# A first stage in quarters: mixed scale and shift chunks, and one-column sums of squares

## The chip, the cores and the metric

One core of a Trainium2 chip runs the whole program: one launch, one inference step. The metric is device time in microseconds (us), the median of repeated runs. A profiled execution of the same program gives the trace from which all durations here are read. Engines are named TensorE (PE; its weight loads are listed as PEld), VectorE (DVE), ScalarE (ACT), GpSimd (POOL) and SyncE (SP, which issues the DMAs of this kernel).

## The reference

One layer of a hybrid decoder, over 1024 prompt tokens and 8 x 4 sample tokens, width 1024, all in float32. What matters here is its beginning, which is the same for prompt and samples:

```
mod = silu(c) @ w_ada + b_ada                      # c: 1 prompt row + 8 sample rows
shift, scale, gate = split(mod, 3)
h = x * rsqrt(mean(x*x) + eps) * g_norm * (1 + scale) + shift
z = h @ w_in                                       # split into mq mk mv, gates, aq ak av, ...
```

After it come an mLSTM branch (q, k, v, two gates per head), an attention branch with a window of 128 and sinks (aq, ak, av), two output products gated by sigmoids of z, the residual with `gate`, and a final norm.

## The kernel before

Tokens lie transposed: `xT[p][k]` is a tile of 128 channels (k = 0..7) by 512 tokens (p = 0, 1), and `xS` holds the 32 sample tokens of all eight k. The matrix `w_in` is used in jobs of 128 columns; `order` lists the jobs, ak and av first, then the four aq. A product is done in a split form: h is kept as a rounded part `h_hi` and a rest `h_lo`, the weights as `wh` and `wl`, and each step of k is three products (wh with h_hi, wh with h_lo, wl with h_hi) that accumulate in PSUM. The columns of tokens are cut in three pieces, `PIECES` (384, 384, and 256 with the 32 samples).

The first stage makes h and, as far as h is ready, the jobs ak and av. Its parts:

- `ada_load`, `ada_rows`, `ada_chunk` (names of tiles: early_h, early_l, ada_, adas_, adat_): one chunk is 512 of the 3072 columns of w_ada, 2 MB. Sixteen passes in four column groups give 512 columns of scale or shift for nine rows, a ScalarE copy brings them to SBUF (`adas`), and four products with a selection matrix turn them (`adat`). Two chunks are scale (sc0, sc1) and two shift (sh0, sh1), each for half of the channels. `scale_done` makes `A` = (1 + scale) * g_norm, `shift_done` makes `B` = shift + bias, for nine rows.
- `x_sq` (xsq, xs, xsum): squares of each token tile, on VectorE and ScalarE in turn, and products with ones that add them over channels in four column groups; a copy to `xsum`.
- `x_rs` (xc, ssq, xr): nine products turn the sums into columns of 128 tokens, and a Newton chain of twelve small VectorE steps (`recip_sqrt`) gives the factors.
- `x_dg`, `x_rows` (xdg, xb): diagonal matrices of the factors and products with ones give each token's factor in all 128 partitions, in PSUM.
- `x_mul`: token tile times A times factor row, one VectorE step; `h_part`: h_hi by adding B (ScalarE, some on VectorE), h_lo on VectorE; `h_plain`: the unsplit h, for the gate products and for storing in DRAM (`hD`); `h_samples`: the same for the samples, with eight small steps for A and B.
- `pair` does the three products of ak and av for some k and one piece; `pair_end` takes the sums out (kr, krr, vT). `gate_piece` (gg) does the eight gate columns from the unsplit h.

The order in the stage is written out by hand in L1511 to L1585. `mm` and `in_order` hold TensorE to it, and the wrappers `V` and `S` hold VectorE and ScalarE to program order as long as their `on` is set; the DMAs stand in program order in one queue with eight outstanding. Behind the stage a planner (`Side`) interleaves attention and gate work with the jobs by due times that are counted in the program, not measured. L213 in the profile is the wrapper's call, L251 `mm`, L239 the DMA issue.

The stage works in halves of k: all sums first, then sc0 and sh0, products of k = 0..3 for the three pieces, with sc1 and sh1 between them, then k = 4..7.

Of the kernel before, what the change touches and what calls it, by code (L numbers as in the profile page):

```python
# [81 lines left out]
def job_columns():  # L82
# [14 lines left out]
    return cols, np.arange(mi, mi + 8), np.concatenate([pair(g) for g in range(4)])  # L97

# [68 lines left out]
def body(tc, a):  # L167
    nc = tc.nc
    with ExitStack() as ctx:
# [100 lines left out]

        cst = cp.tile([128, C_END], F32, name="cst")
        dma(cst[:, :C_TRI], a["cst"][:, :C_TRI])
        ident = cst[:, C_ID:C_ID + 128]
# [4 lines left out]
        cT = ht([128, KT, 9], "cT")  # L278
        dma(cT, a["cT"])
        vec = cp.tile([128, 28], F32, name="vec")  # L280
        dma(vec, a["vec"])
        gmn, bada, gnorm = vec[:, 0:4], vec[:, 4:20], vec[:, 20:28]

        def load_x(p):
            ts = []
            for k in range(KT):
                ts.append(ht([128, 512], f"x{p}_{k}"))
                dma(ts[-1], a["xT"][:, p, k])
            return ts

        xS = ht([128, KT, NS], "xS")
        dma(xS, a["xS"])
        xT = [load_x(p) for p in range(2)]
        xT.append([xS[:, k] for k in range(KT)])

        ct = ht([128, KT, 9], "ct")
        S.activation(ct, cT, AF.Tanh, scale=0.5)
        V.scalar_tensor_tensor(ct, ct, 1.0, cT, op0=ALU.add, op1=ALU.mult)
        c32 = cp.tile([128, KT, 32], F32, name="c32")
        V.memset(c32, 0.0)  # L300
        V.tensor_scalar(c32[:, :, 0:9], ct, 0.5, None, op0=ALU.mult)
# [37 lines left out]
        V.tensor_scalar(b1, bada[:, 8:16], 1.0, None, op0=ALU.add)  # L339
        V.tensor_scalar(gmn, gmn, 0.5, None, op0=ALU.mult)  # L340

        def bc9(v, j):
            return v[:, 4 * j:4 * j + 4].unsqueeze(2).to_broadcast((128, 4, 9))

        def scale_done(j):
# [6 lines left out]
        def shift_done(j):  # L352
            return lambda tp: V.tensor_tensor(B[:, 4 * j:4 * j + 4], tp, bc9(bada[:, 0:8], j), op=ALU.add)

        hD = dp.tile([128, KT, T], F32, name="hD")
        one = cp.tile([128, 128], F32, name="one")
        V.memset(one, 1.0)

        PARTS = (0, 512), (512, 512), (SEQ, NS)

        def x_sq(p):
            n = PARTS[p][1]
            acc = po([128, 512], f"xs{p}")
# [3 lines left out]
            for k in range(KT):  # L367
                if p == 2:
                    sq = sqs[:, k]
                else:  # L370
                    sq = ht([128, 512], "xsq")
                    if k % 2:
                        V.tensor_tensor(sq, xT[p][k], xT[p][k], op=ALU.mult)
                    else:
                        S.activation(sq, xT[p][k], AF.Square)
                j = 32 * (k % 4)
                mm(acc[j:j + 32, :n], one[:, 0:32], sq, start=(k < 4), stop=(k >= 4), share=4)
            sums = ht([128, 512], "xsum")
            S.copy(sums[:, :n], acc[:, :n])
            return sums  # L380

        def x_rs(ps_, sums):
            blocks = [(p, i, min(128, PARTS[p][1])) for p in ps_ for i in range(-(-PARTS[p][1] // 128))]
            nb = len(blocks)
            cols = pg([128, nb], f"xc{ps_[0]}")
            for j, (p, i, m) in enumerate(blocks):
                mm(cols[:m, j:j + 1], sums[p][:, i * 128:i * 128 + m], cst[:, C_S9:C_S9 + 1], start=True, stop=True)
# [99 lines left out]
        def h_hi(k, c0, n, x="h"):  # L487
            ks = k
            if isinstance(k, slice):
                k, ks = k.start, slice(0, 4)  # L490
# [1355 lines left out]
```

## Time and profile before

| | |
|---|---|
| median of 3 runs | 883.22 us (882.14 to 883.58) |
| the profiled execution | 886.0 us, its span 884.2 us |
| TensorE busy | 846.2 us, 96% of the span |
| VectorE, ScalarE, GpSimd busy | 544.3, 381.6, 202.7 us |
| HBM | 106.02 MB read, 39.51 MB written |

The stage in stretches of 5 us (busy us of each engine in the stretch):

| stretch | TensorE | VectorE | ScalarE | DMA, GB/s |
|---|---|---|---|---|
| 5 to 10 | 4.04 | 1.39 | 1.75 | 299 |
| 15 to 20 | 5.00 | 1.48 | 1.92 | 408 |
| 25 to 30 | 4.29 | 3.77 | 0.92 | 392 |
| 30 to 35 | 2.86 | 3.30 | 4.66 | 412 |
| 45 to 50 | 5.00 | 3.76 | 1.95 | 284 |
| 50 to 55 | 3.80 | 4.43 | 5.00 | 32 |
| 60 to 65 | 5.00 | 4.05 | 2.00 | 306 |

How to read the rows of the profile: "start, length, engine, line, operation, out<-in, shapes, count [idle time before it <- what ended that]". Times are us from the start of the span. In rows of a tile the three durations are minimum, median and maximum in ns. In rows of a stretch stand its limits, its length, TensorE's busy time with the number of instructions, the granted clock (1.00 is full), the DMA share and GB/s. Rows of one kind are merged, and their length is then from the first start to the last end or the busy time. A float32 product takes two passes, and each pass is a row of its own.

### The profile page before, as it was taken

The numbers are of one execution on the slowest core, as the hardware profiler recorded it, in microseconds if no ns is written. First come the engines' busy times: TensorE is split into PE (matmuls) and PEld (weight loads), VectorE is DVE, ScalarE is ACT, GpSimd is POOL, SyncE is SP. The second block draws the span as 40 slices with busy tenths as digits, with TensorE's granted clock in tenths as the row PEclk, the third lists the DMA queues.
The fourth block names the chain that finished last, engine by engine and source line by source line (L and its number), as shares of the span: only waits on it lengthen the run. The fifth ranks groups of instructions, "written<-read, shape, count | busy, mean of one in ns | idle before, by whom it ended". The sixth has DMA issues, their size and how long they took to land. (4 is left out here: it accounts for less than half of the span.)

```text
span 884.2 us, 15518 instructions
## 1 busy us (share of the span) xinstructions
PE 846.2 (96%) x5306; PEld 715.8 (81%) x5306; DVE 544.3 (62%) x1496; ACT 381.6 (43%) x986; POOL 202.7 (23%) x208
## 2 busy tenths in 40 slices
PE   6899989999999889999999999999999999999996
PEld 2689988888889879888878877777788999987775
DVE  3786564444758867535655554558756666747785
ACT  3663334445445454645545453434434333223231
POOL 0112210000023423224322223255443302120000
PEclk9999999999999998999999999999999999999998
DMA  8965638364667443344443334464424788452421
GB/s 314 371 227 167 219 128 274 113 223 125 182 164 225 158 127 107 118 161 149 113 136 115 104 124 119 145 174 140 123 93 127 254 284 300 151 155 101 150 78 49
DMA packets 113771, 145.55 MB, mean 165 GB/s; under 512 B 27004, under 2 KB 72444, under 8 KB 113660
## 3 DMA queue, kind: packets, MB, share of 16 engines
q1 hardware_dynamic: 113692, 144.56, 50.7%
q8 instruction: 42, 0.69, 0.3%
q14 instruction: 37, 0.30, 0.1%
HBM read 106.02 MB, written 39.51 MB: 165 GB/s over the span
## 5 line engine op out<-in xcount | busy, mean ns | idle before, releaser
L213 ACT ACTIVATE p<-p,nmx 128x256 f32<-128x256 f32 (+1 forms) x64 | 30.9, 484 | 36.2 <-DVE nmx L213 36.2
L251 PE MATMUL g_w_ao<-ya,wh_w_ao 128*128 128x384 f32 (+1 forms) x192 | 45.5, 322 | 0.9 <-ACT bw L213 0.5
L251 PE MATMUL g_w_mo<-ym_l,wh_w_mo 128*128 128x384 f32 (+1 forms) x192 | 45.7, 323 | 0.0
L213 DVE CUSTOM_DVE_ANT_0 p<-sc,cst,sink 128x256 f32<-128x256 f32 (+1 forms) x64 | 26.1, 463 | 21.7 <-PE sc L251 21.6
L251 PEld LDWEIGHTS g_w_ao<-ya,wh_w_ao 128*128 128x128 f32 x192 | 33.4, 188 | 1.6 <-ACT bw L213 1.0
L213 ACT ACTIVATE fjk<-rows_l 128x512 bf16<-128x512 f32 (+2 forms) x19 | 11.6, 609 | 51.4 <-DVE rows_l L213 25.5
L251 PE MATMUL g_mk<-h_h,wh_mk 128*128 128x384 f32 (+1 forms) x96 | 33.7, 351 | 0.0
L251 PEld LDWEIGHTS g_w_mo<-ym_l,wh_w_mo 128*128 128x128 f32 x192 | 33.5, 188 | 0.0
L251 PE MATMUL g_mv<-h_h,wh_mv 128*128 128x384 f32 (+1 forms) x96 | 33.0, 344 | 0.0
L251 PE MATMUL g_aq<-h_h,wh_aq 128*128 128x384 f32 (+1 forms) x96 | 32.9, 343 | 0.0
L251 PE MATMUL g_mq<-h_h,wh_mq 128*128 128x384 f32 (+1 forms) x96 | 32.5, 338 | 0.0
L251 PE MATMUL g_mk<-h_l,wh_mk 128*128 128x384 f32 (+1 forms) x96 | 31.8, 331 | 0.0
L251 PE MATMUL g_aq<-h_l,wh_aq 128*128 128x384 f32 (+1 forms) x96 | 31.7, 331 | 0.0
L251 PE MATMUL g_mk<-h_h,wl_mk 128*128 128x384 f32 (+1 forms) x96 | 31.6, 329 | 0.0
L251 PE MATMUL g_aq<-h_h,wl_aq 128*128 128x384 f32 (+1 forms) x96 | 31.6, 329 | 0.0
L251 PE MATMUL g_mq<-h_h,wl_mq 128*128 128x384 f32 (+1 forms) x96 | 31.0, 323 | 0.0
L251 PE MATMUL g_mv<-h_h,wl_mv 128*128 128x384 f32 (+1 forms) x96 | 31.0, 323 | 0.0
L251 PE MATMUL g_mq<-h_l,wh_mq 128*128 128x384 f32 (+1 forms) x96 | 31.0, 323 | 0.0
L251 PE MATMUL g_mv<-h_l,wh_mv 128*128 128x384 f32 (+1 forms) x96 | 31.0, 323 | 0.0
L251 PE MATMUL g_w_mo<-ym_l,wl_w_mo 128*128 128x384 f32 (+1 forms) x96 | 31.0, 323 | 0.0
L251 PE MATMUL g_w_ao<-ya,wl_w_ao 128*128 128x384 f32 (+1 forms) x96 | 30.8, 321 | 0.0
L720 POOL TENSOR_TENSOR aq<-aq,cos 128x384 f32<-128x384 f32 (+1 forms) x12 | 15.1, 1254 | 50.2 <-DVE ropet L213 34.5
(1320 smaller groups left out, 2744.3 us busy)
## 6 DMA issues: line engine op xcount, KB each, us to landing
x<-xT SPq DMA_DIRECT2D x16, 256.0 KB, 5.5
early_h<-w_ada SPq DMA_DIRECT2D x8, 512.0 KB, 7.8
early_l<-w_ada SPq DMA_DIRECT2D x8, 512.0 KB, 9.7
hD<-x SPq DMA_DIRECT2D x16, 256.0 KB, 3.3
adar_ga<-w_ada SPq DMA_DIRECT2D x16, 256.0 KB, 5.7
wr_ga<-w SPq DMA_DIRECT2D x16, 256.0 KB, 2.8
hb<-hD SPq DMA_DIRECT2D x16, 256.0 KB, 5.5
wr_gm<-w SPq DMA_DIRECT2D x16, 256.0 KB, 3.1
```

The costliest lines, as they stand in the source:

```text
L213: ins = f(*args, **kw)
L251: in_order(nc.tensor.matmul(out, lhsT, rhs, start=start, stop=stop, skip_group_check=more))
L720: G.tensor_tensor(x, x, cs[0], op=ALU.mult)
```

## The change

- The columns of w_ada are laid out anew on the host (`ada_columns`): a chunk holds 256 columns of scale and the 256 columns of shift of the same channels, so that one chunk gives A and B for two k. There are four such chunks, q0 to q3.
- Loads: token tiles come first, the constants between them; then q0, the first halves of the ak and av weights, q1, q2, the second halves, q3.
- `x_sq`: squares of two tiles are added on VectorE first (groups (0,1), (2,3), (4,5), then 6 and 7 alone), and the sums come from products with the squares as the stationary operand and one column of ones as the moving one, four a group, straight into columns. The copy and the turning products go. First half and samples have one factor chain, the second half another.
- Tokens are multiplied by the factor row alone, before A and B are known (`x_mul`); `h_part` then makes x * A + B in place on ScalarE, copies it to h_hi on ScalarE, and takes the rest on VectorE. `h_plain` goes. `h_samples` has four steps instead of ten.
- `conditions()` (the silu of c and small vectors) comes after the first token products.
- The pairs of jobs run in quarters of two k, with the next chunk's products between them; the weights' split is all on ScalarE and VectorE.
- VectorE and ScalarE are held to program order somewhat longer, the memory banks of some sums change, and two copies (`pick`) move.

The core of it:

```diff
+def ada_columns(w):
+    sh, sc, g = (w[:, i * D:(i + 1) * D] for i in range(3))
+    return np.concatenate([t[:, c:c + 256] for c in range(0, D, 256) for t in (sc, sh)] + [g], 1)
...
+        def tokens_done(q):
             def f(tp):
-                o = A[:, 4 * j:4 * j + 4]
-                V.tensor_tensor(o, tp, bc9(b1, j), op=ALU.add)
-                V.tensor_tensor(o, o, bc9(gnorm, j), op=ALU.mult)
+                k = slice(2 * q, 2 * q + 2)
+                v = lambda t, o=0: t[:, o + 2 * q:o + 2 * q + 2].unsqueeze(2).to_broadcast((128, 2, 9))
+                V.tensor_tensor(A[:, k], tp[:, 0:2], v(b1), op=ALU.add)
+                V.tensor_tensor(A[:, k], A[:, k], v(gnorm), op=ALU.mult)
+                V.tensor_tensor(B[:, k], tp[:, 2:4], v(bada), op=ALU.add)
...
+        def x_sq(cols, j, p, groups):
...
+            for ks in groups:
+                for k in ks:
...
+                        if k in (1, 4):
+                            V.tensor_tensor(sq, xT[p][k], xT[p][k], op=ALU.mult)
+                        else:
+                            S.activation(sq, xT[p][k], AF.Square)
+                    if k > ks[0]:
+                        V.tensor_tensor(sq, sq, before, op=ALU.add)
+                    before = sq
+                for i in range(0, n, 128):
+                    m = min(128, n - i)
+                    c = j + i // 128
+                    mm(cols[:m, c:c + 1], sq[:, i:i + m], one[:, 0:1], start=(ks[0] == i == 0), stop=(k == KT - 1), more=True)
...
-                V.scalar_tensor_tensor(xT[p][k], xT[p][k], A[:, k, 0:1], rows, op0=ALU.mult, op1=ALU.mult)
+                V.tensor_tensor(xT[p][k], xT[p][k], rows, op=ALU.mult)
         def h_part(k, p):
...
+            S.activation(x, x, AF.Identity, bias=B[:, k, 0:1], scale=A[:, k, 0:1])
+            S.copy(hi, x)
+            V.tensor_tensor(lo, x, hi.bitcast(F32), op=ALU.subtract)
...
+        adas = [tokens_ada(0, "h0")]
+        first_load(0)
+        adas += [tokens_ada(1, "h1"), tokens_ada(2, "l1")]
+        first_load(1)
+        adas.append(tokens_ada(3))
+        xc0, xc1 = po([128, 8], "xc0"), po([128, 8], "xc1")
+        groups = (0, 1), (2, 3), (4, 5), (6,), (7,)
+        x_sq(xc0, 4, 2, [(k,) for k in range(KT)])
+        x_sq(xc0, 0, 0, groups)
+        x_sq(xc1, 0, 1, groups[:2])
+        dgs = x_dg((0, 2), *x_rs((0, 2), xc0))
+        rows = {p: x_rows(p, dgs[p]) for p in (0, 2)}
+        x_sq(xc1, 0, 1, groups[2:])
+        x_mul(2, rows[2], None)
+        x_mul(0, rows[0], two[0])
+        conditions()
+        dgs = x_dg((1,), *x_rs((1,), xc1), True)
+        steps(adas[0], 1)
+        rows[1] = x_rows(1, dgs[1])
+        kept = ht([128, 512], "xbs")
+        S.copy(kept, rows[1])
+        x_mul(0, rows[0], two[1])
+        x_mul(1, kept, two[0])
+        run(adas[0])
+        first_split(order[0], 0, V)
+        x_mul(0, rows[0], two[2])
...
+        for q, kk in enumerate(two):
+            more = q < len(two) - 1
...
+            h_part(kk[0], 0)
+            if q == 0:
+                first_split(order[1], 0, V)
+            h_part(kk[1], 0)
+            if q and more:
+                steps(adas[q + 1], 3)
+            pair(kk, 0, acc[0])
+            if q == 0:
+                steps(adas[1], 2)
+            if q and more:
+                run(adas[q + 1])
+            h_part(kk[0], 1)
+            h_part(kk[1], 1)
+            if q == 0:
+                steps(adas[1], 1)
+                x_mul(0, rows[0], two[3])
+            h_samples(kk)
...
+            pair(kk[:1], 1, acc[1])
+            if q == 0:
+                run(adas[1])
+            pair(kk[1:], 1, acc[1])
+            if more:
+                x_mul(1, kept, two[q + 1])
...
+            pair(kk, 2, acc[2])
+            if q == 0:
+                for n in order[:2]:
+                    first_split(n, 1, V)
...
```

More of the change, by code (lines that the diff above doesn't have):

```diff
@@ L1536, in body @@
-        kept = []
-        for p in range(2):
-            kept.append(ht([128, 512], f"xbs{p}"))
-            S.copy(kept[p], rows[p])
-        x_mul(1, rows[1], half[0][1:])
-        x_mul(2, rows[2], None)
-        pair(half[0], 0, acc[0])
-        for k in half[0]:
-            h_part(k, 1)
-        steps(sc1, 3)
-        pair(half[0], 1, acc[1])
-        h_samples(half[0])
-        run(sc1)
-        h_plain(half[0], 0)
-        x_mul(0, kept[0], half[1])
-        steps(sh1, 3)
-        pair((0, 1), 2, acc[2])
```

173 lines of the change are left out of this document (65 added, 108 removed).

## The prediction

> **What bounds the kernel now.** I read the page first, then the timeline of the first 70 us engine by engine, then the stretches table on a 3.41 us grid, then TensorE's waits after 70 us.
>
> ```profile
> span 884.2 us, 15518 instructions
> PE 846.2 (96%) x5306; PEld 715.8 (81%) x5306; DVE 544.3 (62%) x1496; ACT 381.6 (43%) x986; POOL 202.7 (23%) x208
> ```
>
> TensorE is the bound. From its 69.17 us on, its instruction order in the changed program is the old one, so what counts is (1) when the first stage releases that point, and (2) what its few later waits become. The stage (timeline of the kernel before):
>
> ```profile
> 2.60 9.36 SPq L239 DMA_DIRECT2D x<-xT  x16
> 14.39 0.69 DVE L213 TENSOR_TENSOR xsq<-x 128x512 f32<-128x512 f32 x1 [0.66 <-DMA x<-xT]
> 18.82 2.07 PE L251 MATMUL xc<-cst,xsum 128*128 128x1 f32 x17
> 20.95 0.22 DVE L213 TENSOR_SCALAR ssq<-xc 32x1 f32<-32x1 f32 x2 [3.16 <-PE xc L251]
> 23.47 1.01 DVE L213 TENSOR_SCALAR xdg<-cst,xr_y 128x128 f32<-128x128 f32 x5
> 24.89 2.36 PE L251 MATMUL xb<-xdg,one 128*128 128x128 f32 x18
> 25.07 0.20 DVE L213 TENSOR_TENSOR A<-adat_sc,b 128x36 f32<-128x36 f32 x1 [0.59 <-PE adat_sc L251]
> 25.30 0.20 DVE L213 TENSOR_TENSOR A<-A,vec 128x36 f32<-128x36 f32 x1
> 26.07 3.38 DVE L213 SCALAR_TENSOR_TENSOR x<-x,A,xb 128x512 f32<-128x512 f32 x5 [0.57 <-PE xb L251]
> 27.18 1.92 PE L251 MATMUL ada_sh<-early_l,c 128*32 128x512 f32 x16
> 29.18 0.59 ACT L213 COPY adas_sh<-ada_sh 128x512 f32<-128x512 f32 x1 [4.08 <-PE ada_sh L251]
> 29.81 1.06 PE L251 MATMUL adat_sh<-cst,adas_sh 128*128 128x9 f32 x8 [0.70 <-ACT adas_sh L213]
> 33.33 1.28 DVE L213 TENSOR_TENSOR wl_av<-wr_av,wh_av 128x512 fp32r<-128x512 f32 x2
> 33.46 0.69 PE L251 MATMUL g_ak<-h_l,wh_ak 128*128 128x384 f32 x1 [1.10 <-DVE h_l L213]
> 53.63 0.45 PE L251 MATMUL g_ak<-h_l,wh_ak 128*128 128x384 f32 x1 [1.20 <-DVE h_l L213]
> 65.25 0.29 PE L251 MATMUL g_av<-h_h,wl_av 128*128 128x288 f32 x1
> 69.17 0.44 PE L251 MATMUL g_aq<-h_h,wh_aq 128*128 128x384 f32 x1
> ```
>
> From 33.46 to 65.25 TensorE runs the 144 products of ak and av with two of the four scale and shift chunks between them, and waits once, at 53.63. Before 33.46 it waits for a chain: tokens land, squares, sums, factors, rows, chunk, split. The gate products and the queries follow at 69.17 and are unchanged. So the change is worth (start of steady products) + (length of that run) + (effects behind it).
>
> **Start of the run.** Times below are on this trace's axis, at full clock first. Loads: the first token tile is issued where the constants were (0.74 instead of 2.60), and the constants still pass the same queue, so a tile lands 0 to 1.86 us earlier; I take 0.8. In the changed order VectorE reaches the first sums' scaling only after adding the squares of the second half's tiles 2 and 3, so the twelfth tile decides: 14.39 - 0.8 = 13.6, a ScalarE square (0.63, below) and a VectorE add (0.69): 15.0. From ssq to the diagonals is 23.47 - 20.95 = 2.5: 17.5; five diagonals 1.0: 18.5; then a square and an add of tiles 4 and 5 (0.69 each): 19.9. Only now may TensorE do the last three groups of the second half, 3 x 4 one-column products. xc is the nearest row: 18 passes in 2.07, two passes a product, 0.23 each: 2.8, so 22.7 (VectorE has the sample and two token products and the five small condition steps meanwhile, some 2.4 in all, hidden). Again 2.5 to the diagonals: 25.2. The rows take four of xb's nine products (two passes each), 4/9 of 2.36 = 1.05, and a hand-over: 26.35. The second half of the first chunk is queued behind them: 0.96, 27.3. Copy 0.59, four adat products 1.06: 29.1. The three A and B steps 0.65: 29.75. Then VectorE's own order: the split of wl_ak (1.28/2 = 0.64) and two token products (3.38/5 = 0.68 each) stand ahead of the first h_l (0.69): 32.45. That is 1.0 before 33.46. The early parts (tokens scaled first, first tiles first) do not reach the end: a serial VectorE queue with two factor chains, 2 x 3.5 us, replaces one, and it waits for TensorE's products in the middle.
>
> **The clock in that stretch.** This decides. The first sums of the kernel before:
>
> ```profile
> 5.56 0.63 ACT L213 ACTIVATE xsq<-x 128x512 f32<-128x512 f32 x1
> L251 PE MATMUL xs<-xsq,one x4: 1057/1060/1061, 6.2 to 8.0; 128*32 128x512 f32 x4
> L251 PE MATMUL xs<-xsq,one x7: 592/592/617, 10.8 to 12.8; 128*32 128x512 f32 x7
> 5.71:9.13 3.42, 2.89 (x5) 1.00 0.91 294
> 29.60:33.02 3.42, 1.50 (x9) 1.00 1.02 407
> 33.02:36.43 3.41, 2.97 (x9) 0.50 1.03 411
> 114.93:118.34 3.41, 1.05 (x8) 1.00 0.43 158
> 118.34:121.75 3.41, 3.41 (x13) 0.50 0.00 0
> 292.40:295.82 3.42, 1.70 (x12) 1.00 0.30 102
> 31.91 0.19 PEld L251 LDWEIGHTS g_ak<-h_h,wh_ak 128*128 128x128 f32 x1 [1.13 <-ACT h_h L213]
> 33.46 0.29 PEld L251 LDWEIGHTS g_ak<-h_l,wh_ak 128*128 128x128 f32 x1 [1.36 <-DVE h_l L213]
> ```
>
> The second and third rows are the durations (min/median/max, ns) of the same product early and late: 1.06 us, then 0.59. The chip starts at half clock and is released at about 9.1, whatever the clock column says there. The stretch rows give length, TensorE busy, clock: stretches with 1.50 and 1.05 us busy are followed by one at 0.50, one with 1.70 is not. [...] This speaks against the change: the 512-column sums that earned the release, 16 x 2 passes streaming 512 columns each, become 48 products that stream one column and otherwise only load weights. If loads do not count, TensorE is at half clock from 0 until the first chunk, at about 26. No row here shows whether they count; the 1.50 stretch holds 1.06 of adat, which is almost only loads, and still lost the clock, and to that row I lean.
>
> The price: a load of 128 columns at half clock took 0.29 against 0.19, 0.10 more a pass, so 0.43 a product. The first rows (four products and the sample's) and twelve sums: 16 x 0.20, less 0.25 that lies beside VectorE's add = 2.95 late. Then the second rows +0.7, half a chunk +0.85 (0.96 doubled, nearly), adat +0.8; rows and chunk together stream for some 3.5 us, which may release the clock before adat: -0.8. Total +4.5: first steady product at 36.95, 3.5 after 33.46. Bounds: -1.0 (no half clock) and +4.3 (no release). [...]
>
> **Length of the run.** The 144 products are unchanged. Three chunks lie in it instead of two: +2.9 (1.92 + 1.06, less a little overlap). In quarters 1 and 2 the new order puts the next chunk's adat between the first half's and the second half's products, and VectorE has the three A and B steps, which wait for it, ahead of the h_l that the next product needs: adat ends, 0.5, h_l 0.69, less the one product that needs no h_l: 1.0 of idle, twice, +2.0 (0.7 to 1.3 each). Queued behind that wait on VectorE are the samples' steps and the next token products, which have 8 us. The wait of 53.63 goes: -1.2; what is late next there is the round trip just priced. Per quarter ScalarE has 4 x (0.7 + 0.6) + 0.6 = 5.8 and VectorE 8 x 0.69, the samples and A and B, some 7, under TensorE's 8.7 (65.25 - 33.46 less two chunks, the wait and 1.4 of slow start is 23.2; a quarter of it, and a chunk). So x and h copies, the samples and h_part's extra pass cost nothing as long as TensorE is the slower; if not, up to 0.5 a quarter. The slow start after an idle stretch (33.02:36.43 at 0.50) stays. Sum +3.7 (3.3 to 4.3). The VectorE split of ak in place of GpSimd is in the chain above.
>
> **Behind the stage.** One wait loses its cause:
>
> ```profile
> 101.29 0.29 SPq L239 DMA_DIRECT2D m<-m0T  x1
> 103.99 0.18 DVE L213 TENSOR_TENSOR cms<-cms,m 4x32 f32<-4x32 f32 x1 [1.57 <-DMA m<-m0T]
> 104.34 0.40 ACT L213 ACTIVATE p<-p,nmx 128x128 f32<-128x128 f32 x1 [6.19 <-DVE nmx L213]
> 108.30 0.47 ACT L213 ACTIVATE aq<-g_aq 128x384 f32<-128x384 f32 x1
> 117.33 0.55 PE L256 MATMUL pt<-cst,p 128*128 128x128 f32 x3 [2.36 <-DVE row L213]
> ```
>
> m0T's load sits late in SP's queue and VectorE stands 1.57 for it; ScalarE's softmax, its copy of aq at 108.30 and, through VectorE and GpSimd, the 2.36 us wait of TensorE at 117.33 follow, and with that the half-clock stretch 118.34:121.75, worth 1.7. In the changed SP order m0T goes right after the first key store, some 30 us earlier. The reciprocal of den now stands behind a GpSimd product, so only about 0.8 (0 to 1.6) of the 1.57 arrives at 117.33; the stretch then has 1.9 us busy, more than the 1.70 that kept its clock. So -0.8 - 1.7 = -2.5 (0 to -4.1). Elsewhere SP's new order (weights before hD) meets no TensorE wait on a load after 69 us, and I cost it at nothing, up to 1 if the key store comes late.
>
> **Sum.** +3.5 + 3.7 - 2.5 = +4.7. The profiled execution took 886.0 with a span of 884.2, so it would take 890.7; the median of the runs shown is 883.22, and 4.7 on that is 887.9. About 0.2%, 1.8 us, is what a measurement here can tell from no change.
>
> **Rivals.**
> - Full clock: loads count as activity, the stretch of sums is released early. Start -1.0, run +3.7, behind -2.5: +0.2, 883.4. For it: a load-bound queue is busy for most of 6 to 15 us. Against: the 1.50 row.
> - Loads as fast at half clock as at full, only streaming halves: rows +0.8, half a chunk +0.85 on -1.0, so start +0.65: +1.85, 885.1. [...] Against: 0.29 for 0.19.
> - Faster: full clock and the whole of 117.33's wait gone. It decides where ScalarE's copy of aq at 108.30 comes over 2.4 us earlier: then 2.36 + 1.7 = 4.1 go. -1.0 + 3.3 - 4.1 = -1.8, 881.4, and tiles that land the full 1.86 earlier give 880.4. Against: the reciprocal's new place.
> - That the change does not do what it says: the quarters do start with a quarter of the chunks, but hardly sooner; this is the forecast itself.
>
> **How the numbers follow.** Half clock 0.52 (886.5 to 891, its own bounds), full clock 0.25, fast loads 0.10, faster 0.13. The range reaches from the faster rival's 881.3 to 891.0, leaving out 0.1 at each side. Faster than 0.2%: 0.15 (the last rival and a little of full clock); slower: 0.52, most of fast loads and a little of full clock, 0.60; within: 0.25.
>
> **What would show it.** Right: one-column products 0.43 apart until about 25, ada at twice its 1.92 for the first chunk, first steady g_ak<-h_l at about 37, two idle stretches of 1 us ended by h_l after adat, the last av product at about 72.5, no DMA m<-m0T wait. Wrong: products 0.23 apart (full clock), a start before 32, h_l waiting for ScalarE instead, or a 2 us wait for row that stays, which gives 2.5 back.

## The result and the profile after

The changed kernel takes 892.63 us (median of 4 runs, 891.27 to 894.26), the kernel before beside it 882.68 (4 runs); the ratio is 1.0114, 95% interval 1.0092 to 1.0135. On a second chip it took 894.93 against 883.91, ratio 1.012 (1.0099 to 1.014). It is some 10 us slower, where 4.7 was forecast: the sign is right, the time outside the range.

The profiled run took 891.27. The head of the page after:

```profile
span 889.5 us, 15624 instructions
PE 853.7 (96%) x5336; PEld 729.9 (82%) x5336; DVE 544.8 (61%) x1512; ACT 386.2 (43%) x988; POOL 200.3 (23%) x206
```

TensorE's first stage (timeline of the kernel after; columns: start, length, engine, line, operation, out<-in, shapes, count, idle time before and what ended it):

```profile
9.03 10.40 PE L257 MATMUL xc<-one,xsq 128*128 128x1 f32 x48 [0.39 <-DVE xsq L219]
16.06 0.22 DVE L219 TENSOR_SCALAR ssq<-xc 32x1 f32<-32x1 f32 x2 [1.40 <-PE xc L257]
19.30 2.62 PE L257 MATMUL xb<-xdg,one 128*128 128x128 f32 x10
21.84 5.28 PE L257 MATMUL xc<-one,xsq 128*128 128x1 f32 x24
27.05 1.93 PE L257 MATMUL ada_q<-early_h,c 128*32 128x512 f32 x8
27.16 0.16 DVE L219 TENSOR_SCALAR ssq<-xc 128x4 f32<-128x4 f32 x1 [3.07 <-PE xc L257]
29.87 2.08 PE L257 MATMUL xb<-xdg,one 128*128 128x128 f32 x8 [0.89 <-DVE xdg L219]
31.88 1.94 PE L257 MATMUL ada_q<-early_h,c 128*32 128x512 f32 x8
34.52 1.06 PE L257 MATMUL adat_q<-cst,adas_q 128*128 128x9 f32 x8 [0.70 <-ACT adas_q L219]
37.64 0.69 PE L257 MATMUL g_ak<-h_h,wh_ak 128*128 128x384 f32 x1 [2.06 <-ACT h_h L219]
38.54 0.69 PE L257 MATMUL g_ak<-h_l,wh_ak 128*128 128x384 f32 x1 [0.21 <-DVE h_l L219]
56.05 0.44 PE L257 MATMUL g_ak<-h_l,wh_ak 128*128 128x384 f32 x1 [0.89 <-DVE h_l L219]
65.97 0.44 PE L257 MATMUL g_ak<-h_l,wh_ak 128*128 128x384 f32 x1 [0.89 <-DVE h_l L219]
75.24 0.29 PE L257 MATMUL g_av<-h_h,wl_av 128*128 128x288 f32 x1
79.16 0.44 PE L257 MATMUL g_aq<-h_h,wh_aq 128*128 128x384 f32 x1
```

What to see: 48 one-column passes take 10.40, 0.217 each, two a product: 0.43. The rows take 0.26 a pass (18 took 2.36 before, 0.13), half a chunk 1.93 (a whole one took 1.92 before). By these durations TensorE is at half clock until about 34, as the forecast had it; the transposes at 34.52 take 1.06 again, as before. The steady products start at 38.54 instead of 33.46, the two round trips are there with 0.89 each, and the queries start at 79.16 instead of 69.17. So the loss of 10.0 us is complete at the end of the first stage, and by the medians, 9.95 apart, nothing of it comes back behind it. The profiled executions alone could not tell this: their spans are 5.3 us apart in the first pair of profiles (884.2 and 889.5) and 15.0 in the second (880.4 and 895.4).

All runs in one table. Start: first g_ak<-h_l. Run: from there to the end of the last av product. Queries: first g_aq. These three are from each kernel's trace, in us; time and ratio are against runs of the kernel before on the same chip.

| kernel | start | run | queries | median us (before) | ratio, 95% interval |
|---|---|---|---|---|---|
| before, first and second profile | 33.46, 33.78 | 32.1, 32.8 | 69.17, 70.22 | 882.68; 882.16 (one run) | |
| after, first and second profile | 38.54, 39.52 | 37.0, 37.1 | 79.16, 80.21 | 892.63 (882.68); 894.93 (883.91) | 1.0114, 1.012 |
| *from after:* filler | 55.44 | 35.9 | 94.93 | 906.26 (884.74) | 1.0247 (1.0217 to 1.0276) |
| stream128 | 45.61 | 36.7 | 85.91 | 897.97 (883.91) | 1.0153 (1.0130 to 1.0175) |
| round_trip | 39.49 | 36.2 | 79.28 | 895.04 (884.74) | 1.0105 (1.0073 to 1.0137) |
| relief | 38.98 | 38.7 | 81.27 | 897.83 (884.97) | 1.0151 (1.0121 to 1.0182) |
| old_sums | 38.83 | 36.8 | 79.20 | 893.16 (884.97) | 1.0093 (1.0072 to 1.0114) |
| old_sums_warm | 34.44 | 36.7 | 74.73 | 887.73 (883.93) | 1.0035 (1.0020 to 1.0050) |
| warm_trip | 33.28 | 35.3 | 72.18 | 888.97 (883.44) | 1.0064 (1.0044 to 1.0085) |
| *from before:* sums_alone | 39.32 | 32.8 | 75.76 | 887.50 (883.91) | 1.0036 (1.0014 to 1.0058) |
| wait_bare | 38.08 | 32.2 | 74.65 | 889.80 (883.93) | 1.0055 (1.0038 to 1.0072) |
| late10 | 33.35 | 32.7 | 80.00 | 899.73 (883.93) | 1.0159 (1.0134 to 1.0184) |
| m0_early | 33.76 | 32.7 | 70.04 | 885.33 (884.74) | 1.0008 (0.9990 to 1.0027) |
| x_first | 33.16 | 33.3 | 70.08 | 885.06 (884.97) | 1.0006 (0.9987 to 1.0026) |
| keep_warm | 33.54 | 33.1 | 70.30 | 886.28 (883.91) | 1.0018 (1.0000 to 1.0036) |
| keep_warm2 | 33.28 | 31.6 | 68.50 | 884.01 (884.97) | 0.9999 (0.9982 to 1.0016) |
| x_first_warm | 33.53 | 31.6 | 68.73 | 884.31 (883.44) | 1.0008 (0.9989 to 1.0028) |

### The profile page after: what moved, and what is told of

It is laid out like the page before. It is cut to its first block, busy times and chain, and to the rows that moved or that the text cites. A ratio compares the mean times of both kernels' runs of the same rounds, so it can differ in the third digit from the quotient of the medians.

```text
span 889.5 us, 15624 instructions
## 1 busy us (share of the span) xinstructions
PE 853.7 (96%) x5336; PEld 729.9 (82%) x5336; DVE 544.8 (61%) x1512; ACT 386.2 (43%) x988; POOL 200.3 (23%) x206
## 5 line engine op out<-in xcount | busy, mean ns | idle before, releaser
L257 PEld LDWEIGHTS g_w_mo<-ym_l,wh_w_mo 128*128 128x128 f32 x192 | 33.5, 188 | 0.0
L257 PE MATMUL g_w_ao<-ya,wl_w_ao 128*128 128x384 f32 (+1 forms) x96 | 30.8, 321 | 0.0
```

The source lines that it names most:

```text
L257: in_order(nc.tensor.matmul(out, lhsT, rhs, start=start, stop=stop, skip_group_check=more))
```

## Experiments: what is the half clock, and who pays for it?

**filler** and **stream128**: put streamed products between the one-column ones.

```diff
+        fill(2)                       # before the first sums; 512 columns of ones, into an unread bank
...
+                if p < 2:
+                    fill(1)           # before each group; stream128: 256 columns
...
         dgs = x_dg((0, 2), *x_rs((0, 2), xc0))
+        fill(2)
```

In filler the stationary operand is 32 columns wide, in stream128 all 128, and two more of 384 columns stand before the first h_h.

> The changed kernel with products that stream 512 columns of ones into a bank that nothing reads: two before the first sums, one in front of each group of one-column sums, two before the rows. They do no useful work; they only keep TensorE streaming. Clock theory (weight loads with one moving column do not release the clock; streaming does): a one-column product goes from 0.43 to 0.23 us, the first factors are scaled at about 15.0 instead of 16.06, xb takes 0.13 a pass instead of 0.26, the second factors at about 24 instead of 27.16, adat is as now, and the first h_l product starts at 34 to 35 instead of 38.54: -3.5 to -4.5 us for the kernel. Rival 1 (the clock releases by itself at a fixed time, or loads count and the release comes from something else): products still 0.43, and since the fillers themselves take 0.9 to 1.7 us each in TensorE's order, the kernel is 5 to 10 us slower. Rival 2 (the products are not on the path, VectorE's order is): clock released, but start at 38 still: no change.

> The changed kernel with filler products whose stationary operand is 128 columns wide (the fillers of the run named filler had 32): two of 512 columns before the first sums, one of 256 in front of each group of sums, two of 512 before the first rows, two of 384 before the first h_h product. Theory (the clock is released by a stretch in which the whole array works; 32-column products and weight loads with one moving column do not do it): the first two fillers, 3.6 us at half clock, release the clock by about 5; one-column products take 0.23 us from there, xb 0.13 a pass, ada_q 0.12 a pass in quarter 0, and there is no half-clock stretch at the start of the run: first h_l product at 33 to 35, the run 1.2 us shorter, the kernel 5 to 6.5 us faster than the changed kernel. Rival 1 (loads with one column lose the clock again within 3.4 us, in spite of 256 streamed columns a group): start at 36 to 38 and 0 to 2 us faster. Rival 2 (width does not matter, the gate looks at time alone): products at half clock as in the run named filler, 5 to 15 us slower.

The timeline of stream128:

```profile
1.33 3.78 PE L371 MATMUL fill<-one 128*128 128x512 f32 x4 [1.33 <-DVE one L219]
...
6.33 1.22 PE L371 MATMUL fill<-one 128*128 128x256 f32 x2
7.34 1.70 PE L257 MATMUL xc<-one,xsq 128*128 128x1 f32 x8
...
24.27 3.76 PE L371 MATMUL fill<-one 128*128 128x512 f32 x4
27.82 2.48 PE L257 MATMUL xb<-xdg,one 128*128 128x128 f32 x10
...
30.79 0.95 PE L257 MATMUL xc<-one,xsq 128*128 128x1 f32 x8
```

Eight passes take 1.70 until 24 and 0.95 from 30.8 on. So the clock was not released by 3.78 us of streaming from 1.33 on, nor by 18 us in which fillers are 1.2 of every 2.6 us; it was released by fillers and rows in one stretch, 24.27 to 30.30. It was lost again behind the wait of 1.75 us ahead of the second rows, whose eight passes take 2.08 (1.16 in old_sums_warm). In filler it is the same: half clock until fillers and rows follow each other from 32.39 to 38.39 (eight one-column passes 1.87 up to there, 1.05 behind), in spite of 1.9 us of filler in every 3.6. Fillers of 32 and of 128 columns behave alike here, so the theory of stream128 fell, and its first rival with it, since the two fillers ahead of the sums never released the clock. The second rival has the mechanism (half clock as in filler), not the price: 3 us slower than the changed kernel, not 5 to 15. How long a stretch has to be is not shown; here 3.78 us in one piece did not do it and 6.0 us did. Both kernels are slower than the changed kernel, since the fillers cost their own time.

**sums_alone**: the one-column sums alone, put on the kernel before.

```diff
-        sums = {p: x_sq(p) for p in (2, 0, 1)}
-        rs = x_rs((0, 1, 2), sums)
+        cols = po([128, 9], "xc")
+        x_sq(cols, 8, 2, [(k,) for k in range(KT)])          # x_sq and x_rs of the change
+        for p in range(2):
+            x_sq(cols, 4 * p, p, [(k, k + 1) for k in range(0, KT, 2)])
+        rs = x_rs((0, 1, 2), cols)
```

> The kernel before with one part of the change alone: squares of two tiles added, then one-column products (8 for the samples, 32 for the tokens) in place of the 512-column sums, their copies and the nine transposing products. Clock theory: all at half clock, 0.43 each; 1.0 + 32 x 0.43 = 14.8 us from 6, so the factors are scaled at 21 to 22 instead of 20.95, and the clock is then still at half: ada_sc 3.9 instead of 1.9, xb 4.7 instead of 2.4 or part of it; first h_l product 3 to 5 us later than the kernel before, the kernel 2 to 5 us slower. Rival (the clock comes back by itself, or loads count): 0.23 a product, factors at 17 to 18, kernel 2 to 3 us faster.

Its timeline:

```profile
10.13 12.11 PE L251 MATMUL xc<-one,xsq 128*128 128x1 f32 x56 [0.44 <-DVE xsq L213]
22.17 3.64 PE L251 MATMUL ada_sc<-early_h,c 128*32 128x512 f32 x16
26.52 1.88 PE L251 MATMUL adat_sc<-cst,adas_sc 128*128 128x9 f32 x8 [0.70 <-ACT adas_sc L213]
28.24 4.32 PE L251 MATMUL xb<-xdg,one 128*128 128x128 f32 x18
39.32 0.69 PE L251 MATMUL g_ak<-h_l,wh_ak 128*128 128x384 f32 x1 [0.85 <-DVE h_l L213]
```

Sums, chunk, transposes and rows are all at half clock (0.216 a pass, 3.64, 1.88 and 4.32; the kernel before has 1.92 for a chunk, 1.06 and 2.36); the start is 5.5 to 5.9 later. The clock theory holds for this part: used alone it costs the kernel 1.2 to 5.1 us.

**old_sums**: the reverse, the changed kernel with the old 512-column sums in the new order.

```diff
-        x_sq(xc0, 4, 2, [(k,) for k in range(KT)])
-        x_sq(xc0, 0, 0, groups)
-        x_sq(xc1, 0, 1, groups[:2])
-        dgs = x_dg((0, 2), *x_rs((0, 2), xc0))
+        x_sq(2, range(KT))                                   # x_sq and x_rs of the kernel before
+        x_sq(0, range(KT))
+        x_sq(1, range(4))
+        dgs = x_dg((0, 2), *x_rs((0, 2), sums))
```

> The changed kernel with one part undone: the sums of squares as before (32 columns of ones, 512 columns streamed, a copy, transposing products), in the new order, with the new chunks and quarters. Clock theory: the streamed sums release the clock by about 10, so that the transposing products take 0.12 a pass, xb 0.13, ada_q 0.12; the factors of the first half are scaled at 14.5 to 15.5, of the second at 21 to 23 instead of 27.2; first h_l product at 33 to 34.5 instead of 38.5 to 39.5, the kernel 4.5 to 6 us faster than the changed kernel, and still 4 to 6 us slower than the kernel before, which is then the price of the quarters (a chunk more inside the run, two round trips). Rival (the late start comes from the order of the work, two chains of factors one after the other, not from the sums): first h_l product at 37 to 38, 0 to 1 us faster.

The start stayed at 38.83, near the rival's number. But the reason is another one. TensorE's stretches of old_sums (limits, length, busy time, granted clock, DMA share, GB/s) and two rows:

```profile
13.65:17.06 3.41, 2.29 (x15) 1.00 0.94 319
17.06:20.48 3.42, 0.58 (x6) 0.94 0.93 331
20.48:23.89 3.41, 3.41 (x18) 0.50 1.04 416
23.89:27.30 3.41, 2.57 (x16) 0.50 1.03 414
...
30.72:34.13 3.41, 3.32 (x16) 0.56 1.04 404
```

```profile
16.27 1.21 PE L257 MATMUL xc<-cst,xsum 128*128 128x1 f32 x10
20.31 2.64 PE L257 MATMUL xb<-xdg,one 128*128 128x128 f32 x10 [2.84 <-DVE xdg L219]
```

The streamed sums do release the clock: the transposing products at 16.27 take 0.12 a pass. Then TensorE waits 2.84 us for the first factors, with nothing to stream, the clock falls to 0.50, and it stays there till 34. In the kernel before the same wait is filled: ada_sc streams from 20.71 to 23.3 while VectorE makes the factors.

```profile
20.78 2.51 PE L251 MATMUL ada_sc<-early_h,c 128*32 128x512 f32 x13
```

The new order lets the first rows go ahead of every chunk, and so leaves that wait empty.

**old_sums_warm**: old_sums with fillers in the waits only.

```diff
             rows = (pa, pa, pg)[p]([128, 512], f"xb{p}")[:, :n]
+            fill(rows, 512, (3, 2, 0)[p])        # overwritten by the rows
...
+        fill(acc[0][0], 384, 2)                  # before the first h_h
         for q, kk in enumerate(two):
```

> old_sums with filler products of 128 stationary columns in its waits only: three of 512 columns ahead of the first rows (the 2.84 us in which VectorE forms the first factors), two of 512 ahead of the second rows, two of 384 ahead of the first h_h product. Theory (the wait without streamed columns loses the clock, which then stays at half until about 34): rows, second sums, transposing products, ada_q of quarter 0 run at full clock, 0.13, 0.12, 0.12, 0.12 a pass instead of twice that; the second factors at 24 to 25 instead of 27.56, first h_l product at 33.5 to 35 instead of 38.83, no half-clock stretch at the start of the run; the kernel 5 to 6 us faster than old_sums, and 2.5 to 4 us slower than the kernel before. Rival (the late start is VectorE's two chains of factors): first h_l product at 37.5 or later, at most 1 us faster than old_sums.

Its stretches and rows:

```profile
17.06:20.48 3.42, 3.35 (x12) 1.00 0.95 323
20.48:23.89 3.41, 2.68 (x19) 1.00 1.03 408
23.89:27.30 3.41, 3.41 (x20) 1.00 1.03 416
27.30:30.72 3.42, 2.66 (x20) 1.00 1.02 400
```

```profile
17.08 2.84 PE L417 MATMUL xb<-one 128*128 128x512 f32 x6
19.99 1.49 PE L257 MATMUL xb<-xdg,one 128*128 128x128 f32 x10
27.50 1.16 PE L257 MATMUL xb<-xdg,one 128*128 128x128 f32 x8
34.44 0.44 PE L257 MATMUL g_ak<-h_l,wh_ak 128*128 128x384 f32 x1 [0.45 <-DVE h_l L219]
37.96 2.75 PE L257 MATMUL ada_q<-early_h,c 128*32 128x512 f32 x16
```

The clock stays at 1.00 up to the start of the run, the start comes at 34.44, inside the 33.5 to 35 written down, and the ratio falls from 1.0093 to 1.0035, the intervals apart: 0.58% of 884, 5.1 us. So with the old sums the empty waits are what keeps the start late in the new order; products that do nothing, put where TensorE only waited, bring 4.4 us of it back. They delay nothing that was ready, since the rows wait for xdg anyway. Which of the three places counts most was not tried. One part of the theory failed: the run still has a half-clock stretch, only later (its first chunk takes 2.75 instead of 1.92).

**wait_bare**: the mirror, on the kernel before. The first chunk goes behind the rows, so the wait is empty there too.

```diff
-        steps(sc0, 3)
         dgs = x_dg((0, 1, 2), *rs)
-        run(sc0)
         rows = {p: x_rows(p, dgs[p]) for p in range(3)}
+        steps(sc0, 3)
+        run(sc0)
```

> The kernel before with its first chunk (ada_sc and its transposes) moved behind the rows, so that nothing streams while VectorE forms the factors. The move by itself, at full clock, delays A: rows end at about 26.9, chunk 1.92, copy 0.6, transposes 1.06, A 0.6, so the first product with A is at 31.1 instead of 26.1, and the first h_l product 5 us later, at 38.5. Theory (the empty wait of 3.2 us loses the clock): rows at 0.26 a pass (4.7 us instead of 2.4), the chunk partly at half clock too, first h_l product 8 to 10 us later, at 41.5 to 44. Rival (the wait does not matter): rows at 0.13 a pass, first h_l product at 38 to 39.

```profile
24.18 4.01 PE L251 MATMUL xb<-xdg,one 128*128 128x128 f32 x18 [2.89 <-DVE xdg L213]
28.13 1.92 PE L251 MATMUL ada_sc<-early_h,c 128*32 128x512 f32 x16
```

After 2.89 empty us the rows take 4.01 instead of 2.36, as the theory has it; behind the rows the chunk is at 1.92 (granted clock 0.55 from 23.89 to 27.30, 0.95 in the next 3.42 us). The start, 38.08, is the rival's number: the loss of clock costs 1.7 here, and my price of the bare move was too high by some 2 us. The start alone tells nothing apart; the rows do.

## Experiments: the run and its quarters

**round_trip**, **relief** and **warm_trip**: the transposes and A, B steps of quarters 1 and 2 go behind the first tile's products of the second half. relief also gives the scale and shift of tiles 5 and 7 to VectorE; warm_trip is round_trip on old_sums_warm.

```diff
-            if q and more:
-                run(adas[q + 1])
             h_part(kk[0], 1)
...
-            if q == 0:
-                run(adas[1])
+            if more:
+                run(adas[q + 1])
             pair(kk[1:], 1, acc[1])
```

> The changed kernel with the transposes of a chunk and the three A and B steps of quarters 1 and 2 moved behind the first tile's products of the second half (where quarter 0 has them already). Theory: the waits of 0.89 us for h_l at 56.05 and 65.97 go, the run from the first h_l to the last av product shortens from 36.7 to 35.0, the kernel by 1.5 to 1.8 us. Rival: VectorE is the bound inside a quarter, so that the wait comes back one product later or in the next quarter's first h_h: less than 0.5 us.

> round_trip with the scale and shift of tiles 5 and 7 (two of the four tiles of quarter 2, two of the four of quarter 3) on VectorE instead of ScalarE. In round_trip the two waits of 0.89 us went, but the last av product still ended at 75.4: in the last quarter ScalarE works four tiles one after the other, 1.37 us each, from 66.6 to 72.0, and TensorE waits 0.17 us or so for each h_l. Theory (ScalarE is the bound of the last quarter): ScalarE then needs 2 x 1.37 + 2 x 0.6 there, 1.5 us less, and the run ends 1.0 to 1.5 us earlier than in round_trip measured from its first h_l product: 35.0 to 35.4 instead of 36.4. Rival (VectorE's own row of h_l, samples and A and B is as long): the run is as long as in round_trip.

> old_sums_warm with the transposes and the A and B steps of quarters 1 and 2 moved behind the first tile's products, as in round_trip. Theory (quarters: a chunk more in the run, two round trips of 0.89): the two waits go, but ScalarE's four tiles of the last quarter, 1.37 us each, then set the end of the run as they did in round_trip, so that of 1.8 us not more than 0.9 is left: 0 to 0.9 us faster than old_sums_warm, 2.3 to 3.2 us slower than the kernel before. Rival (the last quarter follows the earlier start too): 1.8 us faster than old_sums_warm.

In round_trip the two waits shrink from 0.89 to 0.29 and the products at 65.97 come 2.0 earlier, yet the last av product ends at 75.65, where it ended in the changed kernel (75.53). ScalarE's rows of round_trip say why:

```profile
66.56 0.82 ACT L219 ACTIVATE x<-x,B,A 128x512 f32<-128x512 f32 x1 [2.03 <-DVE B L219]
...
71.52 0.62 ACT L219 CAST h_h<-x 128x512 fp32r<-128x512 f32 x1
```

A and B of the last quarter come at 66.5, 1.2 later than in the changed kernel, and from there ScalarE makes four tiles one after the other, 1.37 each. The end of this run hangs on A and B of the last chunk and 5.6 us of ScalarE, not on TensorE. In the changed kernel the same tiles cost nothing: TensorE runs from 65.97 to 75.53 without an idle stretch. What round_trip's run gained, 0.8 us, is not the waits but its first chunk at full clock (1.92 instead of 2.79), in a part of the program that is the same in both; so that stretch differs by execution, and round_trip's ratio cannot be told from the changed kernel's. relief made it worse (run 38.7 instead of 36.2, of which 0.9 is that chunk at half clock again): with scale and shift on VectorE a tile goes from VectorE to ScalarE to VectorE, and ScalarE waits 1.22 for each such tile, VectorE 0.69. Its theory fell; that the quarter is a chain of hand-overs, not of work, is what it shows. warm_trip's run is 1.4 shorter than old_sums_warm's (0.8 of it the same chunk, 1.92 against 2.75), but its time is not better (intervals overlap), so nothing can be said of its gain in the kernel.

## Experiments: what lies behind the stage

**before_again** and **after_again**: second profiles.

> The kernel before, unchanged: a second profile of it. In the first profile of it TensorE waits 4.17 us at 331 for the product uqv (behind a late read of hb) and then runs 6.8 us at half clock; in the profile of the changed kernel neither is there, and by that point the difference between the two traces falls from 7.2 to 1.5 us, to come back to 5.3. Theory A (an accident of that one execution): both are absent here, the span is 3 us shorter (881), and the traces differ by some 8. Theory B (the change removes them): both are there again and the span is 884.

> The changed kernel, unchanged, on the same chip as the next three: the base for them, and a second profile. From the first runs: 9.9 us slower than before; first h_l product at 38.5, last av product at 75.3. What is open: whether half-clock stretch 37.5 to 44.4 at the start of the run is always there (theory: it hangs on how the idle 35.6 to 37.6 falls, so it may be 3.4 us long instead of 6.8, as it was in round_trip, where it was absent).

Waits of TensorE and the step with m0T (timelines of before_again, then of after and after_again):

```profile
103.53 0.18 DVE L213 TENSOR_TENSOR cms<-cms,m 4x32 f32<-4x32 f32 x1
116.87 0.55 PE L256 MATMUL pt<-cst,p 128*128 128x128 f32 x3 [0.84 <-DVE row L213]
326.90 1.13 PE L251 MATMUL sc<-ukv,uqv 64*128 64x256 f32 x6 [2.40 <-ACT uqv L213]
```

```profile
126.82 0.55 PE L262 MATMUL pt<-cst,p 128*128 128x128 f32 x3 [1.85 <-DVE row L219]
334.78 1.13 PE L257 MATMUL sc<-ukv,uqv 64*128 64x256 f32 x6 [0.77 <-ACT uqv L219]
```

```profile
34.68 1.88 PE L257 MATMUL adat_q<-cst,adas_q 128*128 128x9 f32 x8 [0.70 <-ACT adas_q L219]
341.10 1.13 PE L257 MATMUL sc<-ukv,uqv 64*128 64x256 f32 x6 [2.08 <-ACT uqv L219]
```

In the second execution of the kernel before nothing waits for m0T, the wait for row is 0.84 instead of 2.36, the half-clock stretch behind it is not there (products 0.17 apart, where the first profile has 0.32), and the wait for uqv is 2.40 instead of 4.17; the span is 880.4. So the forecast's -2.5 was read off an accident of one execution. In the changed kernel the wait for row stays, 1.85 in both profiles, and no half-clock stretch follows it (products 0.17 apart in the first). The wait for uqv lies between the two theories, there but shorter; that the change does not remove it is seen in its second profile, which waits 2.08. The changed kernel's start also differs by execution: in the second one even the transposes at 34.68 are at half clock, and the start is 39.52. The slow start of the run is the same in both (first chunk 2.79 and 2.84).

**m0_early** and **late10**, both on the kernel before:

```diff
+        m0 = cp.tile([NH, NB], F32, name="m0")     # m0_early: issued beside the constants at C_TRI
+        dma(m0, a["m0T"])
...
+        for _ in range(12):                        # late10: behind pair_end(2, acc[2])
+            in_order(nc.tensor.matmul(late, one, moving, start=True, stop=True))
```

> The kernel before with one load moved: the 4x8 m0T load is issued with the constants of the attention in the first stage and not in front of its use. Theory (the changed kernel gains behind the stage only since this load has come ahead in SP's queue): cms no longer waits 1.57 us for it, the wait for row at 117.33 shrinks by 0.5 us or goes, the half-clock stretch behind it (118.34 to 121.75) goes: the kernel before gets 1.7 to 2.2 us faster. Rival (the gain has to do with the longer stage, which gives the other loads more time): no change.

> The kernel before with twelve filler products of 512 columns behind the last av products and in front of the gate products: TensorE comes to the gate products some 10 us later, and all loads in flight have that time too. Prediction's view (loads that were late are then there: the wait for row shrinks and a half-clock stretch goes): the kernel becomes 7.5 us slower. Rival (the later waits are not for loads, so nothing is got back): slower by as much as the stage, 9.5 to 10.5 us.

m0_early: the step for cms runs at 98.96 instead of 103.5 to 104, and the wait for row is 1.85; the kernel is as fast as before. So cms was not what that wait hung on. late10: the fillers take 10.46, the queries start at 80.00, and the kernel is 11.8 to 16.3 us slower, more than the delay, not less. Why more is open; the waits for m0T (1.54) and row (2.82) are still there. So this delay got nothing back. Other delays did: sums_alone starts the queries 5.5 to 6.6 us later and costs 1.2 to 5.1, stream128 15.7 to 16.7 later and costs 11.5 to 15.5. What a later stage does to the rest of the kernel therefore goes either way, and why is open; for the change itself the medians show nothing of the 2.5.

**x_first**, **keep_warm**, **keep_warm2**, **x_first_warm**: small parts put on the kernel before. x_first issues the token loads ahead of the constants and runs the condition steps behind the squares. The fillers of keep_warm2 (384 columns) stand before the transposes of sh0, before the first h_h and before the first h_l; keep_warm, as run, had only the one before h_h.

```diff
+        fill(acc0[0], 384)         # in ada_chunk, ahead of adat of sh0, and again ahead of the first h_h
+        fill(acc0[1], 384)         # in pair, ahead of the first h_l product
```

> The kernel before with one part of the change alone: the token loads are issued first, constants, conditions and vectors behind them, and the condition steps run after the squares. Theory (the last token tile sets the chain; SP issues one load in about 0.45 us, and three loads with 118 KB go behind): the last square ends 1.4 us earlier, and with it the factors (20.95 to 21.4 now) and the first h_l product (33.46 to 33.78): -1.2 to -1.6 us. Rival (the transfers, not the issues, are the limit: the first tiles land as late, since the rate only climbs slowly, or ada_sc then waits for its weights or conditions): 0 to -0.5 us.

> The kernel before with two filler products of 128 x 384 (into banks that are overwritten afterwards): one before the first h_h product, one between it and the first h_l product, where TensorE idles 1.04 and 0.85 to 1.10 us. Theory: the stretch 30.7 to 34.1 is then busy for over 2.5 us instead of 1.27 to 1.5 and the clock stays, so that the 3.4 us at half clock at the start of the run (first dozen products 0.32 each instead of 0.17) go: 1.7 us faster, no wait longer. Rival (the fillers push the first h_l product later, or the run then waits for VectorE's next h_l instead): 0 to 0.5 us.

> The kernel before with three filler products of 128 x 384: before the transposes of the first shift chunk, before the first h_h product and before the first h_l product (in keep_warm only one of the two fillers meant was in the kernel, and the half-clock stretch stayed). Theory: the 3.4 us without streamed columns between ada_sh and the run, which hold only adat's loads, are broken into pieces below 1 us, three fillers of 0.64 and 0.2 to 0.45 of the run's own first product; the clock stays, and the first dozen products take 0.17 each instead of 0.32: 1.7 us faster. Rival (the gate wants more than half of a window streamed, as the runs with fillers show for the release): half clock as before, 0 to +0.5 us.

> The kernel before with x_first and keep_warm2 together. Theory (gains of the stage are carried to the end): first h_l product at 32.8 to 33.3, gate products followed by the queries at 68.0 instead of 69.2 to 70.2, the kernel 1.5 to 2 us faster than the kernel before. Rival (TensorE waits for VectorE and loads at fixed times later on, 117 and 294 us, so that an earlier stage only waits longer there): 0 to 0.5 us faster.

The first h_l product of keep_warm and of keep_warm2:

```profile
33.54 0.69 PE L251 MATMUL g_ak<-h_l,wh_ak 128*128 128x384 f32 x1 [0.86 <-DVE h_l L213]
```

```profile
33.28 0.44 PE L251 MATMUL g_ak<-h_l,wh_ak 128*128 128x384 f32 x1 [0.46 <-DVE h_l L213]
```

One filler did not hold the clock (0.69 is half), three did (0.44, granted clock 1.00 from 30.72 to 44.37), and the run got 0.5 to 1.2 shorter than in the kernel before. Of the 1.4 us expected of x_first's loads 0.3 to 0.6 arrived at the start, and in x_first_warm none (33.53). Two rows of x_first show where they were lost:

```profile
19.28 0.22 DVE L213 TENSOR_SCALAR ssq<-xc 32x1 f32<-32x1 f32 x2 [0.63 <-PE xc L251]
21.89 1.05 PE L251 MATMUL ada_sc<-early_h,c 128*32 128x512 f32 x4 [0.23 <-DMA early_h<-w_ada]
```

The tokens did come earlier, and the factors are scaled at 19.28 instead of 20.95. But the first chunk then waits for its own weights and ends at 22.9 instead of 23.3: the rival's second case (ada_sc waits for its weights), not the first (token tiles that land as late). Neither part, nor both together, can be seen in the kernel's time. No version was found that beats the kernel before.

## Why the prediction was wrong, step by step

- **Half clock** (the 0.52 case): right, and with it the sign. One-column products 0.43 (0.43 forecast), rows and half chunk doubled, two round trips of 0.89 (1.0). No run shows weight loads as fast at half clock as at full, which the rival of 885.1 takes: passes of one column, little but a load, took 0.217 in the changed kernel and 0.12 in old_sums.
- **Start of the run**: forecast +3.5, measured +5.1 and +5.7 in the two pairs of profiles. The term that was too small is the first sums. I let the first factors come at 15.0 in both clocks; at half clock the 8 sample products and the 20 of the first half are 1.0 + 8.7 us of TensorE, from 5.5 on and with 0.6 of gaps, and the factors came at 16.06 (+1.05). The second followed at 27.16 instead of 25.65 (22.7 + 2.95), and the way to the rows (2.71 from ssq instead of 2.5) and the slower rows (2.08) made the lag 2.0, of which VectorE's steps behind the transposes gave 0.4 back. No run shows some 3.5 us of rows and chunk as enough to release the clock, the term of -0.8 before adat: behind 3.95 us of them without a gap adat took 1.06 in the first execution and 1.88, half clock still, in the second.
- **The cause of the half clock**: I named the one-column sums alone. old_sums and sums_alone show two causes, each enough by itself: the sums, and an order that leaves the first wait for factors empty. With both repaired (old_sums_warm) the start is 0.7 to 1.0 behind the kernel before. The full-clock rival's -1.0, with one-column sums, could not be tried: nothing here made those run at full clock from the start.
- **Length of the run**: forecast +3.7, measured +4.9 and +4.2. By TensorE's rows the first pair's 4.9 is 3.45 of chunks and transposes, 0.58 of waits and 0.89 of products. The extra chunk (2.6, forecast 2.9) and the round trips (1.78, forecast 2.0) were right. Missing is the slow start, which I kept at the old length: 12 products at 0.32 are followed by a first chunk of 2.79 instead of 1.92, so the half clock lasts 6.8 us instead of 3.4. Why it does stays open: round_trip has the same idle of 2.07 ahead of the first h_h and a first chunk of 1.92. My statement that ScalarE's extra pass costs nothing, TensorE being the slower, held in the changed kernel; it fails in the last quarter of round_trip, where four tiles of 1.37, 5.5 us, begin only with A and B, against 5.9 of products. Its step took 0.81, not 0.7.
- **Behind the stage**: forecast -2.5, measured +0.0 (medians 9.95 apart, stage 9.99) and +1.0 (11.0 and 9.99). This is the largest error, 2.5 to 3.5 us, and the one that put the time outside the range. This step failed in its mechanism: it took TensorE's wait for row, and the half-clock stretch behind it, to hang on m0T's load. before_again has neither that stretch nor a wait for m0T, m0_early has the load early and a wait for row of 1.85, and its time is that of the kernel before (ratio 0.9990 to 1.0027). The forecast itself named the sign, a wait for row of 2 us that stays. What the wait does hang on stays open.

Together: 3.5 + 3.7 - 2.5 = 4.7 against about 5.4 + 4.6 + 0.5 = 10.5; all three terms were too low, so no error hid another. (The faster rival's sum gives 881.4, where the range starts at 881.3; that changes nothing.) The figures of the table do not follow the end of the stage closely: old_sums_warm and wait_bare end it alike (74.7) and differ by 2 us, so some 2 us behind the stage are decided there, and no single trace prices them; by what, stays open.

## What to carry to other kernels

Keep something streaming through the waits of TensorE near the start: a chunk of real work that waits for nothing is what a reorder must not take out of such a wait, and a filler product into a bank that is overwritten anyway can stand in for it (5.1 us in old_sums_warm; too little to measure in keep_warm2). Before a wait of one trace is booked as a gain, profile the kernel before a second time: a wait that differs there by as much as the gain is not a term of the sum. When work is cut into finer pieces, price the last piece by itself, since it has no next piece to hide its chain, as round_trip shows.

## What the runs showed of the hardware

- Weight loads with one moving column left the clock at half for as long as they ran (from 5.5 to 27 us in the changed kernel, with rows between them), and the granted-clock column shows 1.00 in that time; the durations tell (0.217 a pass against 0.12 in old_sums).
- Streaming 1.2 of 2.6 us (stream128) or 1.9 of 3.6 (filler) for 18 and 25 us did not release it, nor did 3.78 us in one piece from 1.33 (stream128) or the two products in filler that end at 4.96; behind 6.0 us in one piece, fillers and rows, it was released in both (eight one-column passes in 0.95 and 1.05 instead of 1.70 and 1.87).
- A wait of 2.84 us (old_sums) or 2.89 us (wait_bare) with nothing to stream lost it: the rows behind took 0.26 and 0.22 a pass instead of 0.13, and the granted clock fell to 0.50 and 0.55.
- 17 runs of the kernel before on one chip took 879.74 to 888.55 us, with mean granted clocks of 0.995 for the two fastest and 0.987 for the slowest; as an estimate from these, 0.8% of 883 is 7 us of the 8.8. Gains of 1 us at a place are therefore seen in traces and not in medians.
